# A Fourier layer folded by the symmetry of cosine and sine

## The chip, the cores and the metric

The program runs on one core of one Trainium2 chip. A core has five engines that matter here: TensorE (PE, matrix products, its weight loads shown apart as PEld), VectorE (DVE), ScalarE (ACT), GpSimd (POOL) and the queue that issues most DMAs (SP). Each runs its own list of instructions strictly in the order in which it was written at build time; between engines they wait by semaphores. The metric is the device time of one execution in microseconds, lower is better.

## The reference

Two layers on x of 512 tokens by 1024 channels in float32. Layer 0 mixes by attention and a recurrence, layer 1 by a Fourier transform over tokens and over the 256 channels of each of four groups. Each mixer is followed by a gated feed-forward of width 2816.

```python
def fourier_mixer(h, w):
    B, S, D = h.shape
    g = h.astype(jnp.float32).reshape(B, S, FOURIER_GROUPS, FOURIER_GROUP_DIM)
    f = jnp.fft.fft2(g, axes=(1, 3), norm='ortho').real
    return f.reshape(B, S, D).astype(h.dtype) @ w

def swiglu(h, wg, wu, wd):
    return (jax.nn.silu(h @ wg) * (h @ wu)) @ wd
...
    for l in range(DEPTH):
        hn = rmsnorm(x, ln_mix_pre[l])
        ...
        else:
            m = fourier_mixer(hn, w_fourier_out[l // 2])
        x = x + rmsnorm(m, ln_mix_post[l])
        hn = rmsnorm(x, ln_ffn_pre[l])
        x = x + rmsnorm(swiglu(hn, w_ffn_gate[l], w_ffn_up[l], w_ffn_down[l]), ln_ffn_post[l])
    return x
```

## The kernel before

Every float32 operand is split into a high and a low part of 12 significant bits (`split`, L100: the high part is a cast on ACT, the low part a subtraction on DVE), and every product is three matrix products, high by high, high by low and low by high (`mm3`, L109 to L111). A token tile is 128 tokens, so there are four (t = 0 to 3); a channel tile is 128 channels.

Weights come through one list of units of 256 columns or rows (`units`), each loaded as two halves of 512 KB by SP into one of three raw buffers (`raws`), then split (L103 on ACT, L106 on DVE) into tiles of a pool of 33 tiles of 128 x 1024 that everything else shares. `next_unit(ahead)` hands out a unit and has the following ones loaded and split. PSUM has eight banks of 128 x 512.

The stages in order are layer 0's mixer and output projection, FFN0, the Fourier mixer, and FFN1. `proj_tok` computes a product as [token, channel]: the row tiles of the contraction in chunks for all four token tiles, and the last of them, the tail, token tile by token tile, so that one token tile ends early and its norm runs beside the products of the next. `post_norm` (L255 to L266) takes the square sums on ACT, the root on POOL (`inv_sqrt`, L209) and the scaling and the residual sum on DVE; `pre_norm` (L236 to L242) normalises the new x, and `turn_x` transposes it on PE for the feed-forward, which needs channels on partitions.

The Fourier mixer takes four steps. `pre_norm_tok` (L764 to L769), called at the end of each of FFN0's token tiles, scales x by its root and splits it. `pos_dft` (L809) transforms over the tokens: cosines in 257 columns, sines in 255. `ch_dft` (L828) transforms over a group's channels into E and O, and `mirror` (L841) makes the columns k and 512-k of the spectrum from E-O and E+O. Last, `proj_tok` multiplies by w_fourier_out, eight row tiles by 1024 channels, with a tail of six, and hands each token tile to `fin1` (both norms). FFN1's first pass (`col_tiles` with `halves`) then works in two halves of 256 tokens, and turns tiles 2 and 3 under them.

The order of each engine's list isn't written out by hand: the framework's scheduler decides it from the program order, the dependences and the buffers in its pools.

## Time and profile before

| | us |
|---|---|
| median of 3 runs | 1058.29 (1057.21 to 1058.57) |
| span of the profiled execution | 1056.6 |
| PE busy in it | 1032.2 |
| DVE, ACT, POOL busy | 480.4, 391.1, 100.3 |
| Fourier mixer, first position product to first product of FFN1 | 607.26 to 685.90 |

The span runs from the first to the last instruction of one execution, so it leaves out what lies around it in a run's time. In the profile a row reads: line, engine, operation, written tile, read tiles, their shapes, count, then busy time, mean length of one in ns, and the idle time ahead of it with what ended it. PE's products overlap, so the distance between two starts, not the length, is what one costs. A row of the timeline begins with its start and its length in us; a row of the window table has the length of the window, the busy time of PE, PEld, DVE, ACT and POOL with their counts, the granted clock, the DMA share and GB/s.

### The profile page before, as it was taken

To read this page: it belongs to the slowest core of one execution; us is meant where nothing else is said; L and a number is where in the kernel's file an instruction comes from. 1 tells how busy PE (TensorE), PEld (TensorE's weight loads), DVE (VectorE), ACT (ScalarE), POOL (GpSimd) and SP (SyncE) were. 2 spreads that over 40 slices of the span, in tenths; PEclk is the share of its full clock that TensorE was granted. 3 is DMA by queue.
4 is the path that set the end of the run, shared out by engine and by line. 5 is a ranking of instruction groups with operands and counts; after the bars stand their busy time and mean duration, and the time that the engine had idled before them with its cause. 6 is when DMAs were issued, how large, how long until landed. Compare 5 with 4: busy or idle time off the path is not lost.

```text
span 1056.6 us, 12277 instructions
## 1 busy us (share of the span) xinstructions
PE 1032.2 (98%) x4913; PEld 857.7 (81%) x4913; DVE 480.4 (45%) x760; ACT 391.1 (37%) x644; POOL 100.3 (9%) x94
## 2 busy tenths in 40 slices
...
GB/s 222 161 107 70 95 46 95 119 41 41 205 153 80 113 108 98 80 81 89 168 111 110 1 65 155 1 80 219 92 127 101 79 80 107 93 80 138 3 1 80
DMA packets 73123, 102.92 MB, mean 97 GB/s; under 512 B 3893, under 2 KB 61290, under 8 KB 73066
## 3 DMA queue, kind: packets, MB, share of 16 engines
...
q8 instruction: 38, 0.62, 0.2%
...
## 4 chain that ended last, share of the span: by engine, by line
PE 94%; DVE 3%; ACT 1%; DMA 1%; issue 1%; POOL 0%; SPq 0%; DVEq 0%; POOLq 0%; ACTq 0%
PE pc L110 15%; PE pc L109 15%; PE pc L111 15%; PE pj L111 10%; PE pj L109 10%; PE pj L110 10%; PE pqk L109 1%; PE psc L559 1%; PE pqk L110 1%; PE pqk L111 1%; PE psc L558 1%; DMA raw<-in_w_in_dram 1%; PE pT L250 1%; PE pyg L109 1%; PE pv L111 1%; PE put L109 1%
## 5 line engine op out<-in xcount | busy, mean ns | idle before, releaser
L106 DVE TENSOR_TENSOR wlo<-raw,whi 128x1024 fp32r<-128x1024 f32 x158 | 190.9, 1232 | 272.2 <-ACT whi L103 221.1
L110 PE MATMUL pc<-hnlo,whi 128*128 128x512 f32 (+1 forms) x768 | 285.1, 372 | 0.0
L109 PE MATMUL pc<-hnhi,whi 128*128 128x512 f32 (+1 forms) x768 | 284.6, 372 | 0.5 <-ACT hnhi L103 0.5
L111 PE MATMUL pc<-hnhi,wlo 128*128 128x512 f32 (+1 forms) x768 | 284.9, 371 | 0.0
L103 ACT CAST whi<-raw 128x1024 fp32r<-128x1024 f32 x164 | 167.4, 1049 | 125.2 <-PE pj L110 31.0
L109 PEld LDWEIGHTS pc<-hnhi,whi 128*128 128x128 f32 x768 | 144.2, 188 | 26.1 <-ACT hnhi L103 1.0
L111 PEld LDWEIGHTS pc<-hnhi,wlo 128*128 128x128 f32 x768 | 144.7, 188 | 25.1
L110 PEld LDWEIGHTS pc<-hnlo,whi 128*128 128x128 f32 x768 | 144.7, 188 | 25.0 <-DVE hnlo L106 0.4
L109 PE MATMUL pj<-whi,gs 128*128 128x512 f32 x352 | 136.9, 389 | 0.0
L110 PE MATMUL pj<-wlo,gs 128*128 128x512 f32 x352 | 136.9, 389 | 0.0
L111 PE MATMUL pj<-whi,gs 128*128 128x512 f32 x352 | 136.9, 389 | 0.0
L93 ACT ACTIVATE gated<-pc 128x512 f32<-128x512 f32 x44 | 26.2, 597 | 268.6 <-PE pc L111 268.6
L729 DVE TENSOR_TENSOR gated<-gated,pc 128x512 f32<-128x512 f32 x44 | 30.2, 686 | 111.4 <-PE pc L111 111.4
L111 PEld LDWEIGHTS pj<-whi,gs 128*128 128x128 f32 x352 | 66.1, 188 | 13.8
L110 PEld LDWEIGHTS pj<-wlo,gs 128*128 128x128 f32 x352 | 66.1, 188 | 13.8
L109 PEld LDWEIGHTS pj<-whi,gs 128*128 128x128 f32 x352 | 66.1, 188 | 13.6
L209 POOL TENSOR_TENSOR r<-m,mhalf 128x1 f32<-128x1 f32 x32 | 17.5, 547 | 552.2 <-DVE m L216 552.2
L260 ACT ACTIVATE y<-pj 128x512 f32<-128x512 f32 x32 | 19.1, 597 | 82.3 <-PE pj L111 82.3
L103 ACT CAST gs<-gated 128x512 fp32r<-128x512 f32 x44 | 25.3, 618 | 52.2 <-PE pj L110 32.2
L106 DVE TENSOR_TENSOR gs<-gated,gs 128x512 fp32r<-128x512 f32 x44 | 28.4, 685 | 31.3 <-ACT gs L103 31.3
L106 POOL TENSOR_TENSOR wlo<-raw,whi 128x1024 fp32r<-128x1024 f32 x12 | 29.7, 2484 | 47.9 <-ACT whi L103 46.8
L93 ACT ACTIVATE p<-p,mx 128x512 f32<-128x512 f32 x32 | 23.1, 723 | 17.6 <-DVE mx L563 17.5
...
## 6 DMA issues: line engine op xcount, KB each, us to landing
raw<-in_w_ffn_gate_dram SPq DMA_DIRECT2D x44, 512.0 KB, 4.1
raw<-in_w_ffn_up_dram SPq DMA_DIRECT2D x44, 512.0 KB, 5.1
raw<-in_w_ffn_down_dram SPq DMA_DIRECT2D x44, 512.0 KB, 3.8
raw<-in_w_in_dram SPq DMA_DIRECT2D x20, 512.0 KB, 3.7
raw<-in_w_mix_out_dram SPq DMA_DIRECT2D x8, 512.0 KB, 3.3
raw<-in_w_fourier_out_dram SPq DMA_DIRECT2D x8, 512.0 KB, 4.3
pos<-in_dft_pos_dram POOLq DMA_DIRECT2D x8, 256.0 KB, 5.7
out_dram<-x SPq DMA_DIRECT2D x8, 256.0 KB, 2.1
```

The costliest lines, as they stand in the source:

```text
L93: ins = A.activation(out_, in_, func, **kw)
L103: A.copy(hi, src)
L106: lo_eng.tensor_tensor(out=lo, in0=src, in1=f(hi), op=ALU.subtract)
L109: T.matmul(ps, lhsT=l[0], rhs=r[0], start=start, stop=False)
L110: T.matmul(ps, lhsT=l[0], rhs=r[1], start=False, stop=False)
L111: T.matmul(ps, lhsT=l[1], rhs=r[0], start=False, stop=stop)
L209: G.tensor_tensor(out=r, in0=m, in1=mhalf[:, 0:1], op=ALU.pow)
L250: T.transpose(pt[:, k * P:(k + 1) * P], xh[:, k * P:(k + 1) * P], ident)
L260: A.activation(ys[h], ps[h], AF.Square, accum_out=ss[h])
L558: T.matmul(ps, lhsT=q_[m][:, t * P:(t + 1) * P], rhs=k_[m], start=True, stop=False)
L559: T.matmul(ps, lhsT=q_[m][sl, t * P:(t + 1) * P], rhs=klo[sl, :], start=False, stop=True)
L729: V.tensor_tensor(out=gated[fc], in0=gated[fc], in1=ps, op=ALU.mult)
```

## The change

The Fourier mixer is computed in a folded form. Cosine is even and sine odd, so within a group channels c and 256-c are combined first, as sums (for the cosines) and differences (for the sines). Rows j and 256-j of w_fourier_out are folded alike (`prep_folded`: the mirrored rows come by a gather DMA, sums and differences are made on DVE and both are split). The map is computed for tokens 0 to 255 as S (from the sums) and T (from the differences); tokens k and 512-k are S-T and S+T (`map_out`). Token tiles 2 and 3 of x are therefore kept in reversed order: written to a scratch in DRAM, gathered back, and stored to the output by a scatter. What doesn't fit the folding (channels 0 and 128, tokens 0 and 256) goes through small products (`pos_rest`, `ch_rest`, `map_rest`) and a row `acc` made on DVE. The gain `g1` of the pre-norm is now a row on all partitions, applied in `pre_norm_tok`. FFN1's first pass is `wide`: six column tiles in halves in place of four.

```diff
 def pre_norm_tok(t):
-        r = pre_stats(t, pair("junk"))
+        h = tile1k("h")
+        r = pre_stats(t, (h[:, 0:S], h[:, S:2 * S]))
+        V.scalar_tensor_tensor(out=h, in0=xt[t], scalar=r, in1=g_pre1[0], op0=ALU.mult, op1=ALU.mult)
+        hv = h.rearrange("p (g c) -> p g c", c=256)
+        w = tile1k("w")
+        wv = w.rearrange("p (z g c) -> p z g c", g=4, c=P)
+        V.tensor_copy(wv[:, :, :, 0:1].rearrange("p z g c -> p g (z c)"), hv[:, :, 0:256:P])
+        V.tensor_tensor(out=wv[:, 0, :, 1:P], in0=hv[:, :, 1:P], in1=hv[:, :, 255:P:-1], op=ALU.add)
+        G.tensor_tensor(out=wv[:, 1, :, 1:P], in0=hv[:, :, 1:P], in1=hv[:, :, 255:P:-1], op=ALU.subtract)
         hi = hn["hi"][:, 2 * t:2 * t + 2, :].rearrange("p a b -> p (a b)")
         lo = hn["lo"][:, 2 * t:2 * t + 2, :].rearrange("p a b -> p (a b)")
-        A.activation(hi, xt[t], AF.Copy, scale=r)
-        V.scalar_tensor_tensor(out=lo, in0=xt[t], scalar=r, in1=f(hi), op0=ALU.mult, op1=ALU.subtract)
-        xs[t] = (hi, lo)
+        for z in range(2):
+            sl = slice(z * S, (z + 1) * S)
+            split(hi[:, sl], lo[:, sl], w[:, sl])
+        hf[t] = (hi, lo)
...
+    def row_index(name, base, first):
+        ix = const.tile([P, 1], mybir.dt.int32, name="ix" + name)
+        G.iota(ix, pattern=[[0, 1]], base=base, channel_multiplier=-1)
+        G.memset(ix[0:1, :], first)
+        rowx[name] = bass.IndirectOffsetOnAxis(ap=ix, axis=0)
+    def gather(tile_, rows_, ix):
+        G.indirect_dma_start(out=tile_, out_offset=None, in_=rows_, in_offset=ix)
+    wsum = []
+    def prep_folded(ap, halves):
+        a, b = (raws.tile([P, 1024], F32, name=nm("raw"), tag="raw") for _ in range(2))
+        nc.sync.dma_start(a, ap[0:P, :])
+        gather(b, w_fourier_out, rowx["w%d" % len(wsum)])
+        G.memset(b[0:1, :], 0.0)
+        for op in (ALU.add, ALU.subtract):
+            w = tile1k("wf")
+            V.tensor_tensor(out=w, in0=a, in1=b, op=op)
+            if op == ALU.add:
+                wsum.append(w)
+            hi, lo = tile1k("whi", F32R), tile1k("wlo", F32R)
+            split(hi, lo, w)
+            halves.append((hi, lo))
...
+        if t >= 2:
+            nc.sync.dma_start(scratch[(t - 2) * P:(t - 1) * P, :], xt[t])
...
-    for n in range(2):
-        w = tile1k("ch", F32R)
-        G.dma_start(w, dft_ch[n])
-        chT.append(w)
+    chT = [tile1k("ch", F32R) for _ in range(2)]
+    def chw(i):
+        return chT[i // 8][:, (i % 8) * P:(i % 8 + 1) * P]
+    for z in range(2):
+        for n in range(2):
+            G.dma_start(chw(2 * z + n), dft_ch[n, :, z * 256:z * 256 + P])
+    G.memset(f(chT[0][:, S:]), 0.0)
+    G.memset(f(chT[1]), 0.0)
+    for g in range(4):
+        G.dma_start(chw(4 + g)[32 * g:32 * g + 1, :], dft_ch[0, 0:1, 512:512 + P])
+        for q in range(3):
+            G.dma_start(chw(8 + g)[:, 32 * q + g:32 * q + g + 1], dft_ch[0, :, P:P + 1])
+        G.memset(f(chw(12)[32 * g:32 * g + 1, g:g + 65:32]), 1.0 / 16.0)
+    G.memset(f(chw(13)[:, 0:1]), 1.0)
+    xr = [xt[0], xpool.tile([P, D], F32, name=nm("x2"), tag="x2"), xpool.tile([P, D], F32, name=nm("x3"), tag="x3"), xt[1]]
+    gather(xr[1], scratch, rowx["c"])
+    gather(xr[2], scratch, rowx["d"])
...
+    def pos_dft(g, ts):
+        if g not in ups:
+            ups[g] = bank("put")
+        ps = ups[g]
+        for t in ts:
+            for z, (r0, o0, n) in enumerate(((0, 0, 258), (257, 256, 256))):
+                o = (z * 4 + g) * P
+                mm3(ps[:, o0:o0 + n], [a[:, o:o + P] for a in hf[t]], [a[:, r0:r0 + n] for a in posT[t]],
+                    t == 0 and z == 0, t == 3 and z == 1, skip_group_check=True)
+    def pos_rest(ts):
+        if "r" not in ups:
+            ups["r"] = bank("put")
+        ps = ups["r"]
+        for t in ts:
+            mm3(ps[:, 0:258], [a[:, S:2 * S:4] for a in hf[t]],
+                [a[:, 0:258] for a in posT[t]], t == 0, t == 3)
...
+    def ch_dft(g):
+        pe, po = bank("pe"), bank("po")
+        ut, ur = uts[g], uts["r"]
+        mm3(pe[:, 0:258], (chw(0), chw(1)), [a[:, 0:258] for a in ut], True, False)
+        for a in ur:
+            T.matmul(pe[:, 0:258], lhsT=chw(4 + g), rhs=a[:, 0:258], start=False, stop=a is ur[1])
+        mm3(po[:, 0:256], (chw(2), chw(3)), [a[:, 256:512] for a in ut], True, True)
+        e, o = fe[g], fo[g] = pair("fe", F32R), pair("fo", F32R)
+        split(*[a[:, 0:256] for a in e], pe[:, 0:256])
+        e256[g] = sm("e256")
+        V.tensor_copy(e256[g], pe[:, 256:257])
+        for a in o:
+            G.memset(f(a[:, 0:1]), 0.0)
+        split(*[a[:, 1:256] for a in o], po[:, 1:256])
...
+    def ch_rest():
+        ps = bank("pe")
+        n = 0
+        for g in (0, 1, 2, 3, "r"):
+            for a in uts[g]:
+                T.matmul(ps[:, 0:258], lhsT=chw(8 + (4 if g == "r" else g)), rhs=a[:, 0:258], start=n == 0, stop=n == 9)
+                n += 1
+        e256["r"] = sm("e256")
+        V.tensor_copy(e256["r"], ps[:, 256:257])
+        A.copy(fr[:, 0:256], ps[:, 0:256])
+        V.tensor_tensor(out=fr[64:P, 0:256], in0=ps[64:P, 0:256], in1=f(fr[64:P, 0:256]), op=ALU.subtract)
...
-    proj_tok(range(8), lambda k: fT[k], 2, 6, fin1, turn_x)
+    acc = tile1k("acc")
+    V.tensor_scalar(out=acc, in0=wsum[0], scalar1=e256[0], scalar2=None, op0=ALU.mult)
+    for g in range(1, 4):
+        V.scalar_tensor_tensor(out=acc, in0=wsum[g], scalar=e256[g], in1=acc, op0=ALU.mult, op1=ALU.add)
+    V.scalar_tensor_tensor(out=acc[0:32, :], in0=w128[0:32, :], scalar=e256["r"][0:32, :], in1=acc[0:32, :], op0=ALU.mult, op1=ALU.add)
+    acch, accl = tile1k("acc", F32R), tile1k("acc", F32R)
+    split(acch, accl, acc)
+    psm = [[[bank("pm"), bank("pm")] for _ in range(2)] for _ in range(2)]
+    def map_part(i, h, g):
+        sl = slice(i * P, (i + 1) * P)
+        d = slice(h * S, (h + 1) * S)
+        ps = psm[i]
+        mm3(ps[0][h], [a[:, sl] for a in fe[g]], [a[:, d] for a in wf[g][0]], g == 0, False)
+        mm3(ps[1][h], [a[:, sl] for a in fo[g]], [a[:, d] for a in wf[g][1]], g == 0, g == 3 and i == 1)
+    def map_rest(i, h):
+        sl = slice(i * P, (i + 1) * P)
+        d = slice(h * S, (h + 1) * S)
+        T.matmul(psm[i][0][h], lhsT=fr[:, sl], rhs=wr[:, d], start=False, stop=True)
+        if i == 0:
+            for a in (acch, accl):
+                T.matmul(psm[i][1][h], lhsT=chw(13), rhs=a[:, d], start=False, stop=a is accl)
+    def map_out(i):
+        y = [pair("ya"), pair("yc")]
+        for h in range(2):
+            A.copy(y[0][h], psm[i][1][h])
+            V.tensor_tensor(out=y[1][h], in0=psm[i][0][h], in1=y[0][h], op=ALU.add)
+            V.tensor_tensor(out=y[0][h], in0=psm[i][0][h], in1=y[0][h], op=ALU.subtract)
+        for z in range(2):
+            t = (z, 3 - z)[i]
+            post_norm(t, y[z], g_post1)
+            pre_norm(t, g_fpre1)
+    for i in range(2):
+        for g in range(2):
+            for h in range(2):
+                map_part(i, h, g)
+    for i in range(2):
+        for h in range(2):
+            for g in (2, 3):
+                map_part(i, h, g)
+            map_rest(i, h)
+            if i and h:
+                turn_x(0)
+                turn_x(1)
+        map_out(i)
+    deferred.extend((lambda: turn_x(2), lambda: turn_x(3)))
...
+        if t in (1, 2):
+            G.indirect_dma_start(out=out, out_offset=rowx[("oc", "od")[t - 1]], in_=xt[t], in_offset=None)
+            return
...
-    ffn(1, after1, 4)
+    ffn(1, after1, 4, wide=True)
```

The change moves instructions on every engine. Three places follow, with the rows of each engine's list in their order (line, operation, written tile, read tiles, shape; x2 is two like rows).

**ACT at the end of FFN0.** Before: pj are the products of FFN0's token tiles, y the square of `post_norm`, junk that of `pre_norm_tok`, hnhi the high part of the normalised tile.

```order
L260 ACTIVATE y_4549,ss_4550<-pj_3923 128x512
L260 ACTIVATE y_4549,ss_4551<-pj_3924 128x512
L222 ACTIVATE junk_4566,ss_4567<-x_79 128x512
L222 ACTIVATE junk_4566,ss_4568<-x_79 128x512
L260 ACTIVATE y_4615,ss_4616<-pj_3925 128x512
L768 ACTIVATE hnhi_4564<-x_79,r_4575 128x1024
L260 ACTIVATE y_4615,ss_4617<-pj_3926 128x512
L222 ACTIVATE junk_4630,ss_4631<-x_80 128x512
L222 ACTIVATE junk_4630,ss_4632<-x_80 128x512
L260 ACTIVATE y_4679,ss_4680<-pj_3927 128x512
L768 ACTIVATE hnhi_4564<-x_80,r_4639 128x1024
```

After: h takes the place of junk, w holds the sums and differences of `pre_norm_tok`, of which the differences come from POOL (L827).

```order
L302 ACTIVATE y_4639,ss_4640<-pj_3949 128x512
L302 ACTIVATE y_4639,ss_4641<-pj_3950 128x512
L264 ACTIVATE h_4656,ss_4657<-x_81 128x512
L264 ACTIVATE h_4656,ss_4658<-x_81 128x512
L302 ACTIVATE y_4712,ss_4713<-pj_3951 128x512
L104 CAST hnhi_4654<-w_4668 128x512 x2
L302 ACTIVATE y_4712,ss_4714<-pj_3952 128x512
L264 ACTIVATE h_4727,ss_4728<-x_82 128x512
L264 ACTIVATE h_4727,ss_4729<-x_82 128x512
L302 ACTIVATE y_4783,ss_4784<-pj_3953 128x512
L104 CAST hnhi_4654<-w_4739 128x512 x2
L302 ACTIVATE y_4783,ss_4785<-pj_3954 128x512
```

The second square of y of the next tile stands behind the two high casts of the tile ahead of it, and those read w, which DVE and POOL have to finish first; before, it stood behind one cast that read x.

**POOL from the end of FFN0 on.** Before: r are roots of the norms, ch the constants of the channel transform, gpre a gain row.

```order
L209 TENSOR_TENSOR r_4688<-m_4685,mhalf 128x1
L209 TENSOR_TENSOR r_4703<-m_4700,mhalf 128x1
L209 TENSOR_TENSOR r_4752<-m_4749,mhalf 128x1
L116 DMA gpre_5105<-in_ln_ffn_pre_dram 128x1024
L799 DMA ch_4771<-in_dft_ch_dram 128x1024
L209 TENSOR_TENSOR r_4767<-m_4764,mhalf 128x1
L799 DMA ch_4773<-in_dft_ch_dram 128x1024
L209 TENSOR_TENSOR r_5234<-m_5231,mhalf 128x1
```

After (the first w is tile 2's difference, the second tile 3's; ch_4891 and ch_4892 are the constants, x_812 the gathered token tile).

```order
L827 TENSOR_TENSOR w_4810<-h_4798 128x4x127
L251 TENSOR_TENSOR r_4864<-m_4861,mhalf 128x1
L117 DMA gpost_5156<-in_ln_mix_post_dram 128x1024
L251 TENSOR_TENSOR r_4879<-m_4876,mhalf 128x1
L827 TENSOR_TENSOR w_4882<-h_4870 128x4x127
L881 DMA ch_4891<-in_dft_ch_dram 128x128 x4
L882 MEMSET ch_4891 128x512
L883 MEMSET ch_4892 128x1024
L885 DMA ch_4891<-in_dft_ch_dram 1x16x8
L887 DMA ch_4892<-in_dft_ch_dram 128x1 x3
L888 MEMSET ch_4892 1x3
L885 DMA ch_4891<-in_dft_ch_dram 1x16x8
```

The loads of the constants now stand behind the difference of the last tile; there are twenty of them, and 27 rows up to the first gather of x.

**DVE and PE at the entry of FFN1.** Before, on DVE: wlo_5168 to wlo_5192 are the low parts of FFN1's first two units; the m, y, x and xn rows are the norms of token tile 0.

```order
L106 TENSOR_TENSOR wlo_5168<-raw_5165,whi_5167 128x1024
L106 TENSOR_TENSOR wlo_5174<-raw_5171,whi_5173 128x1024
L106 TENSOR_TENSOR wlo_5186<-raw_5183,whi_5185 128x1024
L106 TENSOR_TENSOR wlo_5192<-raw_5189,whi_5191 128x1024
L215 TENSOR_SCALAR m_5230<-ss_5226 128x1
L216 TENSOR_SCALAR m_5231<-ss_5227,m_5230 128x1
L265 SCALAR_TENSOR_TENSOR y_5225<-pj_5109,r_5234,gpost_5103 128x512
L265 SCALAR_TENSOR_TENSOR y_5225<-pj_5110,r_5234,gpost_5103 128x512
L266 TENSOR_TENSOR x_79<-x_79,y_5225 128x512 x2
L215 TENSOR_SCALAR m_5245<-ss_5241 128x1
L216 TENSOR_SCALAR m_5246<-ss_5242,m_5245 128x1
L242 SCALAR_TENSOR_TENSOR xn_5240<-x_79,r_5249,gpre_5105 128x512 x2
```

After, on DVE: the norms of the last token tile (x_813), and behind them wlo_5477, the low part of FFN1's first half unit.

```order
L257 TENSOR_SCALAR m_5451<-ss_5447 128x1
L258 TENSOR_SCALAR m_5452<-ss_5448,m_5451 128x1
L307 SCALAR_TENSOR_TENSOR y_5446<-yc_5411,r_5455,gpost_5156 128x512 x2
L308 TENSOR_TENSOR x_813_4921<-x_813_4921,y_5446 128x512 x2
L257 TENSOR_SCALAR m_5466<-ss_5462 128x1
L258 TENSOR_SCALAR m_5467<-ss_5463,m_5466 128x1
L284 SCALAR_TENSOR_TENSOR xn_5461<-x_813_4921,r_5470,gpre_5158 128x512 x2
L107 TENSOR_TENSOR wlo_5477<-raw_5474,whi_5476 128x1024
L107 TENSOR_TENSOR wlo_5483<-raw_5480,whi_5482 128x1024
L107 TENSOR_TENSOR wlo_5489<-raw_5486,whi_5488 128x1024
```

The four splits that stood ahead of the norms now stand behind the norms of all four token tiles. On PE, before, the last product of the projection (pj) and the first of FFN1 (pc):

```order
L109 MATMUL pj_5116<-whi_5006,f_5100 128x512
L110 MATMUL pj_5116<-wlo_5007,f_5100 128x512
L111 MATMUL pj_5116<-whi_5006,f_5100 128x512
L109 MATMUL pc_5473<-hnhi_5107,whi_5167 128x256
L110 MATMUL pc_5473<-hnlo_5108,whi_5167 128x256
L111 MATMUL pc_5473<-hnhi_5107,wlo_5168 128x256
```

On PE, after, the end of the map (pm), with the row acc, and the first of FFN1:

```order
L1009 MATMUL pm_5209<-acc_5202,ch_4892 128x512
L1009 MATMUL pm_5208<-acc_5203,ch_4892 128x512
L1009 MATMUL pm_5209<-acc_5203,ch_4892 128x512
L292 MATMUL pT_5382<-ident,xn_5315 128x128 x4
L292 MATMUL pT_5389<-ident,xn_5315 128x128 x4
L292 MATMUL pT_5396<-ident,xn_5343 128x128 x4
L292 MATMUL pT_5403<-ident,xn_5343 128x128 x4
L110 MATMUL pc_5510<-hnhi_5160,whi_5476 128x256
L111 MATMUL pc_5510<-hnlo_5161,whi_5476 128x256
L110 MATMUL pc_5511<-hnhi_5160,whi_5476 128x256
L111 MATMUL pc_5511<-hnlo_5161,whi_5476 128x256
L112 MATMUL pc_5510<-hnhi_5160,wlo_5477 128x256
```

The products with acc stand at the end of the map, the turns pT of tiles 0 and 1 stand between the map and FFN1, and pc's third kind of product (L112) waits for wlo_5477.

149 lines of the change are left out of this document (81 added, 68 removed).

## The prediction

> **What bounds the kernel now.** I read the page's busy times first, then the chain that ended last, then the window table of the stage that changes.
>
> ```profile
> PE 1032.2 (98%) x4913; PEld 857.7 (81%) x4913; DVE 480.4 (45%) x760; ACT 391.1 (37%) x644; POOL 100.3 (9%) x94
> PE 94%; DVE 3%; ACT 1%; DMA 1%; issue 1%; POOL 0%; SPq 0%; DVEq 0%; POOLq 0%; ACTq 0%
> 606.00:622.00 16.00, 16.00 (x73) 13.23 (x72) 6.72 (x12) 5.25 (x11) 2.74 (x5) 1.00 0.32 99
> 622.00:645.00 23.00, 23.00 (x148) 20.98 (x147) 19.83 (x35) 16.93 (x35) 0.00 (x0) 1.00 0.30 93
> 645.00:660.00 15.00, 15.00 (x68) 12.43 (x67) 5.52 (x6) 4.68 (x7) 0.00 (x0) 1.00 0.46 140
> 660.00:700.00 40.00, 39.76 (x239) 35.22 (x238) 22.66 (x46) 13.75 (x38) 4.94 (x9) 1.00 0.04 14
> ```
>
> TensorE (PE) is the chain, and in the Fourier stage (window columns: length, then PE, PEld, DVE, ACT, POOL) it is busy without a gap. So each product removed is worth its step, but only as long as PE still finds its operands: DVE is busy for 19.83 of 23 us in the second window already.
>
> **What the arithmetic saves.** The step from one product to the next is read off PE's timeline (start, length).
>
> ```profile
> 607.26 0.39 PE L109 MATMUL put<-pos,hnhi 128*128 128x512 f32 x1
> 607.48 0.39 PE L110 MATMUL put<-pos,hnhi 128*128 128x512 f32 x1
> ...
> 623.58 0.28 PE L109 MATMUL pe<-u,ch 128*128 128x258 f32 x1
> 623.69 0.28 PE L110 MATMUL pe<-u,ch 128*128 128x258 f32 x1
> ...
> 685.68 0.39 PE L111 MATMUL pj<-whi,f 128*128 128x512 f32 x1
> 685.90 0.28 PE L109 MATMUL pc<-hnhi,whi 128*128 128x256 f32 x1
> ```
>
> A 512-column product takes 0.227 us, a 256- or 258-column one 0.12. Before: 96 x 0.227 + 96 x 0.12 + 192 x 0.227 = 76.9 us. After: positions 96 + 12 and channels 32 + 10 of at most 258 columns, 150 x 0.12 = 18.0, and the map's 96 + 8 of 512 columns, 23.6; together 41.6. PE is spared **35.3 us**. The wide first pass of FFN1 adds back 48 products' worth of halves: 96 x 0.12 - 48 x 0.227 = 0.6.
>
> **What the other engines add.** These rows price the new work (mean ns of one).
>
> ```profile
> L106 DVE TENSOR_TENSOR wlo<-raw,whi 128x1024 fp32r<-128x1024 f32 x158 | 190.9, 1232 | 272.2 <-ACT whi L103 221.1 <-issue 40.3 <-PE pc L110 10.4
> L769 DVE SCALAR_TENSOR_TENSOR hnlo<-x,r,hnhi 128x1024 fp32r<-128x1024 f32 x4 | 5.1, 1284 | 7.7 <-ACT hnhi L768 7.7
> L106 DVE TENSOR_TENSOR hnlo<-pT,hnhi 128x512 fp32r<-128x512 f32 x24 | 15.5, 682 | 9.3 <-ACT hnhi L103 9.3
> L488 DVE TENSOR_SCALAR gate<-th 128x512 f32<-128x512 f32 x8 | 3.1, 428 | 0.0
> L103 ACT CAST whi<-raw 128x1024 fp32r<-128x1024 f32 x164 | 167.4, 1049 | 125.2 <-PE pj L110 31.0 <-DMA raw<-in_w_ffn_gate_dram 23.9 <-PE pj L111 21.4
> L103 ACT CAST hnhi<-pT 128x512 fp32r<-128x512 f32 x24 | 13.2, 583 | 16.6 <-PE pT L250 16.6
> L497 POOL TENSOR_TENSOR gate<-gate,th 128x512 f32<-128x512 f32 x8 | 16.2, 2062 | 8.6 <-ACT th L93 8.6
> L471 POOL TENSOR_TENSOR gate<-gate,xc 128x512 f32<-128x512 f32 x8 | 12.3, 1557 | 36.2 <-ACT gate L93 36.2
> L789 POOL DMA_DIRECT2D pos<-in_dft_pos_dram x4 | 2.1, 528 | 278.4 <-PE pj L111 266.6 <-DVE gs L106 11.9
> ...
> masks.py:197 POOL MEMSET ident<- 128x128 f32 x1 | 0.2, 205 | 0.3 <-POOLq L915 0.3
> ```
>
> And the last norm before FFN1, from the timelines of ACT, POOL and DVE:
>
> ```profile
> 686.16 0.60 ACT L260 ACTIVATE y<-pj 128x512 f32<-128x512 f32 x1 [2.42 <-PE pj L111]
> ...
> 691.66 0.56 POOL L209 TENSOR_TENSOR r<-m,mhalf 128x1 f32<-128x1 f32 x1 [1.55 <-DVE m L216]
> ...
> 692.25 1.42 DVE L242 SCALAR_TENSOR_TENSOR xn<-x,r,gpre 128x512 f32<-128x512 f32 x2 [0.75 <-POOL r L209]
> ```
>
> From the start of the second square of y, the second root r is done after 6.1 us and the normalised tile after 7.5.
>
> **Step 1, into the Fourier stage.** FFN0's products still end near 607.3, as before; I put 0.8 on top, since four casts of gs now stand behind a weight cast that waits for PE. In the new order the last token tiles' tails are 24 products each (four row tiles, two halves, three), not 36, so tile 0 ends 3 x 24 x 0.227 = 16.3 us ahead of that, at 591.8; its second square starts at about 592.5. ACT's rows in the section on the change show what follows: tile t+1's second square stands behind tile t's two hi casts, and these wait for the difference on POOL (L827). One turn is 6.1 (to r) + 1.28 (h, as L769) + POOL's subtraction of 508 elements + two casts at 0.58. The subtraction lies between 1.56 and 2.06 by the two POOL rows; I take 1.8, their middle. That gives 10.3 us a tile, so tile 3's second square starts at 623.4, POOL's last subtraction ends at 632.7, and its halves are split by 634.6. Before, nothing there waited: the norms hid behind products that are now spent. PE's own products up to there (tiles 0 to 2: 72 and 9) are 81 x 0.12 = 9.7 us of the 26.5 after 608.1, so it idles about **17 us**.
>
> In the Trainium skill, "SBUF — State Buffer", Who interferes with whom, says that a DVE instruction with two SBUF inputs contends with a GpSimd instruction that reads SBUF, and that the loser blocks for the whole instruction. L826 (DVE) and L827 (POOL) are such a pair, so by it I would add up to one 0.68 per tile, 2.7 in all; the two POOL rows above already span 0.5 us for one shape, so the sum keeps their middle.
>
> **Step 2, the channel constants.** POOL's rows show its 20 ch loads and two wide memsets behind the last L827, where before the two loads stood among the norms. From 632.7: four loads at 0.55, memsets of 512 and 1024 elements (bounds: 0.2 each by the 128-element row, 1.6 by that row times eight; I take 1.2 for both), then four groups of four loads and a memset at 2.3: the last is issued at 645.3.
>
> ```profile
> lv<-in_lambda_q_dram SPq DMA_DIRECT2D x2, 32.0 KB, 3.4
> lv<-in_lambda_k_dram SPq DMA_DIRECT2D x2, 32.0 KB, 5.0
> raw<-in_w_fourier_out_dram SPq DMA_DIRECT2D x8, 512.0 KB, 4.3
> pos<-in_dft_pos_dram POOLq DMA_DIRECT2D x8, 256.0 KB, 5.7
> ```
>
> Landing takes 3.4 to 5.7 by the nearest rows (3.4 taken, the smallest load's), so ch_rest's products start at 648.7 and end at 650. DVE's copy of e256 from them stands ahead of the sum wf of weight unit 2: wf, lo, wf, lo at 1.23, with ACT's 1.05 casts between, run to 656.8. The second wf ends at 654.5 and frees the raws, and only then unit 3 loads (4.3, plus 0.55 to issue its gather; a gather is not in the trace, so 3.3 to 5.7). Its wf, cast, lo, wf, cast, lo end at 666.5. The accumulator row follows on DVE: one 0.86 (twice L488) and four of 1.28, then cast and lo: 674.8. PE's order has the four acc products after every other product of the map, so the map ends at **E = 675**. PE itself needs only 23.6 us for it.
>
> **Step 3, into FFN1.** This is the largest term. Before, tiles 0 to 2 were normalised under the products of the tiles behind them, FFN1's first weights were split ahead of the norms, and the first FFN1 product followed the last pj after 0.22 us (rows at 685.68 and 685.90). After, all four token tiles come out of the same last products, and DVE's rows show the first lo of FFN1 (wlo_5477) behind the fourth xn. From E: two copies from PSUM and the sums and differences, then the chain of tile 0, 10.5; tile 1 behind it 7.5; tile 3, with its own four sums and differences and tile 0's and 1's hnlo between, 10; tile 2, 7; wlo 1.2. That is 36.2, and PE does some 2 us of turns and four products within it. The DVE work alone bounds it from below: 8 x 0.68 for sums, per tile 2 x (0.75 + 0.68 + 0.75) and 0.36, four hnlo of 0.68 and one wlo are 28 us; waits between engines at the same hops, up to 40. FFN1 resumes at 711.2 instead of 685.9: **25.3 us later**, though PE had 35.3 less to do. Its later weights keep up: three raws are loaded by then, and a half unit costs DVE 1.23 against 24 x 0.12 = 2.9 of products.
>
> ```profile
> L242 DVE SCALAR_TENSOR_TENSOR xn<-x,r,gpre 128x512 f32<-128x512 f32 x24 | 17.0, 749 | 10.5 <-POOL r L209 7.1 <-DMA gpre<-in_ln_mix_pre_dram 3.2
> L265 DVE SCALAR_TENSOR_TENSOR y<-pj,r,gpost 128x512 f32<-128x512 f32 x32 | 22.6, 747 | 11.2 <-POOL r L209 11.2
> L266 DVE TENSOR_TENSOR x<-x,y 128x512 f32<-128x512 f32 x32 | 20.5, 682 | 0.0
> 13.00:18.00 5.00, 4.27 (x18) 3.98 (x19) 4.22 (x8) 3.69 (x8) 0.56 (x1) 1.00 0.85 301
> ...
> 13.53 0.41 PE L110 MATMUL pv<-wlo,hnhi 128*128 128x256 f32 x1
> ...
> 17.46 0.41 PE L109 MATMUL pv<-whi,hnhi 128*128 128x256 f32 x1
> 17.68 0.41 PE L110 MATMUL pv<-wlo,hnhi 128*128 128x256 f32 x1
> ...
> 18.10 0.28 PE L109 MATMUL pv<-whi,hnhi 128*128 128x256 f32 x1
> 18.22 0.28 PE L110 MATMUL pv<-wlo,hnhi 128*128 128x256 f32 x1
> ```
>
> The last six rows are the kernel's own start. The window's granted clock reads 1.00 there, yet from 13.53 to 18.10 a 256-column product steps by 0.22 us and from then on by 0.12. Those 4.6 us do the work of 2.5, so I add **2 us** for the same after the long idle (0 to 2.1). The Trainium skill, "TensorE: Matmul & The Clock Gate", Part 1: The HAM clock gate, states half clock after an idle window and about 3.4 us of work to leave it; by its figure I would estimate 1.7 here, and nothing at the shorter gaps where PE waits for a norm anyway.
>
> The remaining edits cost nothing that PE waits for: the iotas lie at the start, ahead of a wait for the first DMAs; the x2 and x3 rows go out on SP during the norms and are gathered some 20 us before map_out reads them; the scattered stores of tiles 1 and 2 lie beside the tail's products, and tile 3 still leaves through SP. If that cover fails, each is one transfer of 4 to 6 us by the two rows of 512 and 256 KB above.
>
> **The sum.** 25.3 + 0.6 + 2 - 0.5 (four FFN1 products done early) = 27.4. The profiled span is 1056.6 us and the median of the runs 1058.29, so 1.7 lies around it: 1084.0 as a span, **1085.7** as a time, 2.6% slower.
>
> **The rivals.**
> - *The arithmetic decides, faster.* Were every wait hidden, 1058.3 - 35.3 + 0.6 = 1023.6. It needs the new idle time to stay below 35 us; steps 1 and 3 alone make 17 and 34. Its place is FFN1's entry: it decides where the four norms end behind running products again, so that step 3's 36.2 shrink below 10. For it speaks only that DVE and ACT are under half busy over the span. 0.08.
> - *FFN1 starts on two tiles.* If PE resumed when tiles 0 and 1 are turned (E + 20) and the second pair ran under FFN1's first half, it would be 16 us earlier, 1069. DVE's order speaks against it; a weight split that comes earlier than its row would be needed. 0.12.
> - *POOL's loads are slower, still slower than forecast.* 12 loads of one element per partition and three gathers have no like in the trace. At 5.7 instead of 3.4 to land, and 1 us instead of 0.55 to issue, step 2 grows by 2.3 + 20 x 0.45 = 11.3: 1097. It decides once E depends on ch_rest, as it does here by 650. 0.15.
> - *It does not do what it says.* If 258-column products with strided weights cost the 512-column step, 150 x 0.107 = 16 us come back, mostly in idle time: up to 1095. The ch rows, already 258 wide at 0.12, speak against it. 0.03.
>
> The forecast has 0.62 (its own range 1074 to 1096). To hold 8 in 10, the range reaches to the second and third rivals: 1066 to 1100. About 0.2% is what a measurement here can tell from no change: faster 0.08, within it 0.03, slower 0.89.
>
> **What would show it.** Right: PE waits at the Fourier entry for hnhi casts in turns of about 10 us; POOL busy with issues until 645; acc the last map products at 675; DVE busy and PE empty for over 30 us before pc, released by wlo. Wrong: pc starting while post-norms still run, POOL's subtraction or loads far off the rows, or PE without gaps in the first 30 us after FFN0.

## The result, and the profile after

| | before | after |
|---|---|---|
| median of four runs each, us | 1058.43 (1057.21 to 1059.18) | 1089.15 (1088.79 to 1091.72) |
| ratio to before | | 1.0298 (1.0283 to 1.0313) |
| span of the profiled execution, us | 1056.6 | 1089.9 |
| PE busy in it, us | 1032.2 | 1015.0 |

The changed kernel is 3.0% slower. The profiled execution of after is the slowest of its four runs (1091.72), so 2.6 us of its span are not in the median.

First the page of after: busy time, share of the span and instructions of each engine, then PE's busy tenths in 40 slices of 27.2 us and the clock granted to it.

```profile
PE 1015.0 (93%) x4831; PEld 843.5 (77%) x4831; DVE 501.5 (46%) x786; ACT 387.6 (36%) x636; POOL 143.0 (13%) x201
...
PE   5999999999999999999999777179999999999997
...
PEclk9998999999999999999999989579999999999999
```

PE is busy 17.2 us less, yet the span is 33.3 longer, so PE's idle time has grown by 50.5 us. The slices say where: from the 23rd to the 27th, 599 to 736 us, and worst in the 26th, 681 to 708, where PE is busy for a tenth and the clock falls to 5 tenths. The window table shows two stretches of it (length, then PE, PEld, DVE, ACT, POOL, clock, DMA share, GB/s):

```profile
608.00:640.00 32.00, 19.69 (x105) 18.41 (x104) 18.56 (x38) 10.72 (x28) 12.71 (x16) 0.83 0.20 58
...
680.00:720.00 40.00, 9.51 (x40) 8.45 (x41) 29.39 (x55) 17.60 (x44) 5.04 (x9) 0.50 0.12 36
```

Before, PE was busy in every microsecond from 606 to 660. Now 12 of 32 us are missing in the first window, and 30 of 40 between 680 and 720, where DVE works 29.39 us and the granted clock is 0.50. PE's timeline of after names the waits (start, length, row, then the idle time ahead of it and what ended it):

```profile
609.98 0.28 PE L110 MATMUL put<-pos,hnhi 128*128 128x258 f32 x1
...
615.50 0.36 PE L110 MATMUL put<-pos,hnhi 128*128 128x258 f32 x1 [4.63 <-issue]
...
625.98 0.61 PE L110 MATMUL put<-pos,hnhi 128*128 128x258 f32 x1 [1.89 <-ACT hnhi L104]
...
636.77 0.60 PE L110 MATMUL put<-pos,hnhi 128*128 128x258 f32 x1 [5.57 <-ACT hnhi L104]
...
651.68 0.50 PE L110 MATMUL pm<-whi,fo 128*128 128x512 f32 x1 [0.57 <-POOL fo L949]
...
677.51 2.48 PE L1009 MATMUL pm<-acc,ch 128*128 128x512 f32 x4 [4.21 <-ACT acc L104]
689.70 1.94 PE L292 MATMUL pT<-ident,xn 128*128 128x128 f32 x8 [9.71 <-DVE xn L284]
696.80 1.97 PE L292 MATMUL pT<-ident,xn 128*128 128x128 f32 x8 [5.16 <-DVE xn L284]
713.01 0.58 PE L110 MATMUL pc<-hnhi,whi 128*128 128x256 f32 x1 [14.25 <-ACT whi L104]
...
715.62 0.58 PE L112 MATMUL pc<-hnhi,wlo 128*128 128x256 f32 x1 [1.38 <-DVE wlo L107]
```

PE waits in turns for the high part hnhi of the next tile, then for acc, for the normalised tiles xn, and for the first high and low part of a weight (whi, wlo). The row at 615.50 names no releaser, but ACT's casts of tile 1's hnhi end 0.1 us ahead of it (614.26 and 1.14 us). These rows give the books of the stage. From the first position product (609.98) to the third product of FFN1 (715.62) pass 105.6 us, of which PE needs 41.6 by the prediction's count. The other 64 us lie in four stretches ("lost" is the length less the products' own time; it holds waits and slow steps):

| stretch | from, to | length | products | lost |
|---|---|---|---|---|
| token tiles 0 to 2, waiting for tile 3 | 609.98, 636.77 | 26.8 | 81 of 0.12 | 17.1 |
| tile 3, channel transform, first map products | 636.77, 651.68 | 14.9 | 69 of 0.12, 6 of 0.227 | 5.3 |
| rest of the map, with the products of acc | 651.68, 679.99 | 28.3 | 98 of 0.227 | 6.1 |
| norms and turns ahead of FFN1 | 679.99, 715.62 | 35.6 | (four, and the turns) | 35.6 |

The stage began 2.7 us later than before (607.26) and released FFN1's third product 29.5 later (686.13 before, two steps behind 685.90). From there to the end of the span 374.3 us pass, 370.5 before.

### The profile page after: what moved, and what is told of

It is laid out like the page before. It is cut to its first block, busy times and chain, and to the rows that moved or that the text cites. A ratio compares the mean times of both kernels' runs of the same rounds, so it can differ in the third digit from the quotient of the medians.

```text
span 1089.9 us, 12286 instructions
## 1 busy us (share of the span) xinstructions
PE 1015.0 (93%) x4831; PEld 843.5 (77%) x4831; DVE 501.5 (46%) x786; ACT 387.6 (36%) x636; POOL 143.0 (13%) x201
## 5 line engine op out<-in xcount | busy, mean ns | idle before, releaser
L107 DVE TENSOR_TENSOR wlo<-raw,whi 128x1024 fp32r<-128x1024 f32 x150 | 181.4, 1232 | 263.9 <-ACT whi L104 218.8
L110 PE MATMUL pc<-hnhi,whi 128*128 128x512 f32 (+1 forms) x784 | 288.6, 370 | 14.6 <-ACT whi L104 14.2
L112 PE MATMUL pc<-hnhi,wlo 128*128 128x512 f32 (+1 forms) x784 | 289.0, 369 | 1.4 <-DVE wlo L107 1.4
L104 ACT CAST whi<-raw 128x1024 fp32r<-128x1024 f32 x156 | 159.5, 1049 | 119.2 <-PE pj L111 33.5
L110 PEld LDWEIGHTS pc<-hnhi,whi 128*128 128x128 f32 x784 | 148.7, 190 | 39.6 <-ACT whi L104 14.6
L112 PEld LDWEIGHTS pc<-hnhi,wlo 128*128 128x128 f32 x784 | 149.1, 190 | 26.1 <-DVE wlo L107 1.7
L111 PEld LDWEIGHTS pc<-hnlo,whi 128*128 128x128 f32 x784 | 149.4, 191 | 24.4 <-DVE hnlo L107 0.2
L112 PE MATMUL pj<-whi,gs 128*128 128x512 f32 x352 | 136.2, 390 | 0.0
L110 PEld LDWEIGHTS pj<-whi,gs 128*128 128x128 f32 x352 | 66.1, 188 | 15.7 <-ACT gs L104 2.2
L112 PEld LDWEIGHTS pj<-whi,gs 128*128 128x128 f32 x352 | 66.1, 188 | 14.4 <-DVE gs L107 0.7
L858 POOL DMA_DIRECT2D pos<-in_dft_pos_dram x8 | 4.5, 566 | 270.9 <-PE pj L112 263.1
L292 PE MATMUL pT<-ident,xn 128*128 128x128 f32 x96 | 15.7, 313 | 26.0 <-DVE xn L284 25.1
L302 ACT ACTIVATE y<-pj 128x512 f32<-128x512 f32 x24 | 14.3, 595 | 62.4 <-PE pj L112 62.4
```

What stands on the lines that cost most here:

```text
L104: A.copy(hi, src)
L107: lo_eng.tensor_tensor(out=lo, in0=src, in1=f(hi), op=ALU.subtract)
L110: T.matmul(ps, lhsT=l[0], rhs=r[0], start=start, stop=False, **kw)
L111: T.matmul(ps, lhsT=l[0], rhs=r[1], start=False, stop=False, **kw)
L112: T.matmul(ps, lhsT=l[1], rhs=r[0], start=False, stop=stop, **kw)
L292: T.transpose(pt[:, k * P:(k + 1) * P], xh[:, k * P:(k + 1) * P], ident)
```

## The experiments

The theory: the arithmetic is saved as counted, but the order of the program sets three serial chains in its place, one at the entry (a norm per token tile), one at the map's end (acc behind the last folded weights), one ahead of FFN1 (four norms, and only then the first split of a weight). Its rivals: that an edit of another kind costs the time (the wide pass, the buffers), and that DVE's sheer work, not the order, fills the gap. All times are medians, with the ratio to the kernel before on the same chip. That kernel took 1059.00 us beside e1 to e4, 1058.57 beside e5 to e8 and 1058.77 beside e9 to e11, against 1058.43 beside the change, so differences between kernels hold to 1 or 2 us.

| kernel | median, us | ratio |
|---|---|---|
| e1: acc left out | 1084.10 | 1.0240 (1.0223 to 1.0257) |
| e2: two units split ahead | 1080.97 | 1.0205 (1.0188 to 1.0222) |
| e3: differences on DVE | 1084.34 | 1.0243 (1.0226 to 1.0260) |
| e5: norms in pairs | 1088.07 | 1.0278 (1.0262 to 1.0293) |
| e6: first pass not wide | 1088.60 | 1.0280 (1.0264 to 1.0295) |
| e4: all three chains mended | 1056.91 | 0.9985 (0.9976 to 0.9995) |
| e7: e4, norms in pairs, one low part on POOL | 1054.18 | 0.9955 (0.9942 to 0.9969) |
| e8: before, with four raw buffers | 1059.75 | 1.0009 (1.0000 to 1.0018) |
| e9: e7, not wide | 1063.97 | 1.0049 (1.0032 to 1.0065) |
| e10: e7, splits not ahead | 1069.85 | 1.0107 (1.0091 to 1.0124) |
| e11: e7, entry as changed | 1065.17 | 1.0058 (1.0041 to 1.0075) |

### One chain at a time

**e1** leaves out the row acc and its four products.

```diff
-    acc = tile1k("acc")
...
-    split(acch, accl, acc)
...
-        if i == 0:
-            for a in (acch, accl):
-                T.matmul(psm[i][1][h], lhsT=chw(13), rhs=a[:, d], start=False, stop=a is accl)
```

> Leaves out the row acc: its five DVE operations, its cast and low part, and its four products (the output of tokens 0 and 256 lacks their term). Theory (the map's end waits for acc): in the profile of the changed kernel PE has done every other product of the map by 673.3 and waits 4.21 us for acc, whose products end at 679.5. Without them the map ends about 6 us earlier and the time is 1089 - 6 = 1083 (1081 to 1085). Rival (the map's end is set by the weights of unit 3 alone and acc lies beside them): 1088 to 1089.5.

It came out at 1084.1: acc, last in the map's order, costs about 5 us. In its profile the map ends at 675.41 instead of 679.99, although tile 3's first product comes 2.1 us later than in after (638.90), for a reason that wasn't tried; so 5 us may be somewhat too little.

**e2** splits FFN1's first two units ahead of the last products of the map, so that they stand ahead of the four norms on ACT and DVE.

```diff
+    for _ in range(2):
+        prep_one()
     for i in range(2):
         for h in range(2):
             for g in (2, 3):
                 map_part(i, h, g)
```

> Hands out FFN1's first two units ahead of the map's end in the program, so that their four splits stand ahead of the first copy of map_out on ACT and DVE. Theory (PE waits at FFN1's entry for a weight split that stands behind four norms): tiles 0 and 1 were normalised at 697.4, the split came at 715.6. The fourth raw can be loaded only when the first split frees its buffer (about 680), lands 4 to 5 us later, and the copies behind its cast start at 685.5 instead of 679.6, so the norms come 6 us later: products of FFN1 resume at about 705, and the rest of the first half waits a little for the third unit. 1089 - 9 = 1080 (1077 to 1083). Rival (the norms of all four tiles are needed before FFN1 can work): no gain or a loss, 1089 to 1095.

It came out at 1080.97, 8 us less than the change. PE's timeline of e2:

```profile
695.38 1.94 PE L292 MATMUL pT<-ident,xn 128*128 128x128 f32 x8 [15.83 <-DVE xn L284]
702.48 1.97 PE L292 MATMUL pT<-ident,xn 128*128 128x128 f32 x8 [5.16 <-DVE xn L284]
704.27 1.01 PE L110 MATMUL pc<-hnhi,whi 128*128 128x256 f32 x3
...
718.70 0.39 PE L110 MATMUL pc<-hnhi,whi 128*128 128x256 f32 x1 [1.64 <-ACT whi L104]
```

The first turn is now 5.7 us later than in after (689.70), since DVE does four splits first, but FFN1 follows the second turn directly, at 704.27: the 14.25 us of idle time ahead of 713.01 in after are gone. Those were an order, not a lack of an engine.

**e3** moves the differences of the entry from POOL to DVE.

```diff
-        G.tensor_tensor(out=wv[:, 1, :, 1:P], in0=hv[:, :, 1:P], in1=hv[:, :, 255:P:-1], op=ALU.subtract)
+        V.tensor_tensor(out=wv[:, 1, :, 1:P], in0=hv[:, :, 1:P], in1=hv[:, :, 255:P:-1], op=ALU.subtract)
```

> The difference of channels c and 256-c (L827) on DVE instead of POOL. Theory (the turn of 10.3 to 11.1 us per token tile into the Fourier stage is one chain through POOL's 1.8 us): sum and difference take 2 x 0.68 on DVE, and the first high cast need not wait for the second; each of four tiles gains about 1.0, the turn is 9.5, and all behind it moves with it: 1089 - 4 = 1085 (1084 to 1087). By the Trainium skill's page on SBUF, where a DVE instruction with two SBUF inputs blocks beside a GpSimd one, the gain would be larger by what POOL loses to DVE now. Rival (the entry is bound by FFN0's products or by the constants on POOL): 1088 to 1090.

It came out at 1084.34. DVE's timeline of e3 shows one turn of the chain and the next:

```profile
608.41 1.29 DVE L821 SCALAR_TENSOR_TENSOR h<-x,r,gpre 128x1024 f32<-128x1024 f32 x1 [0.73 <-POOL r L251]
...
609.81 0.68 DVE L826 TENSOR_TENSOR w<-h 128x508 f32<-128x508 f32 x1
610.41 0.68 DVE L827 TENSOR_TENSOR w<-h 128x508 f32<-128x508 f32 x1
...
617.94 1.29 DVE L821 SCALAR_TENSOR_TENSOR h<-x,r,gpre 128x1024 f32<-128x1024 f32 x1 [0.73 <-POOL r L251]
```

The difference takes 0.68 us here against 1.79 on POOL, and a turn 9.5 us (608.41 to 617.94) against the 10.3 to 11.1 of after. ACT's order changed with it (both squares of the next tile stand ahead of the high casts), so the gain isn't the 1.1 us of the instruction alone. PE gets tile 3 at 630.46 instead of 636.77; 1.4 of these 6.3 us lie ahead of the stage (first position product at 608.56 instead of 609.98). The spans of the two profiled executions differ by 9.2 us, twice the 4.8 of the medians, so times read off one execution can't be set against a median to the microsecond.

**e6** takes the wide first pass back.

```diff
-    ffn(1, after1, 4, wide=True)
+    ffn(1, after1, 4)
```

> FFN1's first pass in halves over four column tiles again, not six; all else as in the changed kernel. Theory (PE resumes only behind all four norms, so the wide pass covers nothing here and only costs its halves): 48 products of 512 columns in place of 96 of 256 save 0.6, and the third unit is needed later: 1089 - 0.6 = 1088.4 (1086.5 to 1089.2). Rival (the wide pass covers the norms of tiles 2 and 3, as it is built to): 1092 to 1096.

At 1088.6 it can't be told from the change: where FFN1 starts with all weights late, the wide pass buys nothing.

### A miss: the norms in pairs

**e5** writes the two norms of `map_out` stage by stage, so that each engine finds the second token tile's step beside the first's.

```diff
-        for z in range(2):
-            t = (z, 3 - z)[i]
-            post_norm(t, y[z], g_post1)
-            pre_norm(t, g_fpre1)
+        for z in range(2):
...
+            rs.append(inv_rms(ss[0], ss[1], D))
+        for z in range(2):
+            for h in range(2):
...
+                V.tensor_tensor(out=xt[ts[z]][:, sl], in0=xt[ts[z]][:, sl], in1=ys[z][h], op=ALU.add)
+        for z in range(2):
+            xs2[z] = pair("xn")
+            rs[z] = pre_stats(ts[z], xs2[z])
...
```

> In map_out alone, the norms of the two token tiles of a half are written stage by stage (both squares and roots, then both residual sums, and so on) instead of one tile behind the other; nothing else differs from the changed kernel. Theory (the 36 us from the map's end to FFN1 are one in-order chain on DVE, part of it waits for roots and squares): in the changed kernel DVE is idle for about 8 of the 35 us between its first sum (680.22) and the split (715.58), in waits of 0.2 to 0.75; in pairs about half of them are covered by the other tile. 1089 - 4.5 = 1084.5 (1082 to 1087). Rival (DVE's and ACT's work itself fills the chain): 1088 to 1090.

It came out at 1088.07, where the rival had it. The window of e5 from the end of the map to the first low part of FFN1, and PE's timeline:

```profile
679.10:712.60 33.50, 5.01 (x20) 4.05 (x20) 26.73 (x54) 17.12 (x43) 7.00 (x9) 0.55 0.05 16
```

```profile
691.23 1.94 PE L292 MATMUL pT<-ident,xn 128*128 128x128 f32 x8 [12.32 <-DVE m L257]
693.40 1.84 PE L292 MATMUL pT<-ident,xn 128*128 128x128 f32 x8 [0.23 <-DVE xn L1042]
...
712.64 0.58 PE L112 MATMUL pc<-hnhi,wlo 128*128 128x256 f32 x1 [2.97 <-DVE wlo L107]
```

DVE works 26.73 of these 33.5 us (27.56 of 36 in after, 680 to 716), so pairing can only squeeze the 7 us in which it waits, and it took two of them. The first turn comes later (691.23 against 689.70), the second at once behind it. So for the chain ahead of FFN1 both theories hold a part: DVE's work fills it, and only the order decides whether PE has products meanwhile.

### All three mended

**e4** mends the three chains at once. The gain is applied to x before the root is known, and the root goes into the high cast and the low part, as before the change; the differences are on DVE; the term of acc goes to PE as 26 products (column 256 as one more column of each left operand) in place of a row made on DVE; three units are split ahead of the map's end, with a fourth raw buffer and one tile less in the pool; the loads of pos come later.

```diff
-NTILE = 33
-NRAW = 3
+NTILE = 32
+NRAW = 4
...
-        V.scalar_tensor_tensor(out=h, in0=xt[t], scalar=r, in1=g_pre1[0], op0=ALU.mult, op1=ALU.mult)
+        V.tensor_tensor(out=h, in0=xt[t], in1=g_pre1[0], op=ALU.mult)
...
-            split(hi[:, sl], lo[:, sl], w[:, sl])
+            A.activation(hi[:, sl], w[:, sl], AF.Copy, scale=r)
+            V.scalar_tensor_tensor(out=lo[:, sl], in0=w[:, sl], scalar=r, in1=f(hi[:, sl]), op0=ALU.mult, op1=ALU.subtract)
...
-        if k < 4 and calls[0] >= 32 + 4 * k:
+        if k < 4 and calls[0] >= 40 + 8 * k:
...
+        if i == 0:
+            mm3(ps[1][h], [a[:, 256:384] for a in fe[g]], [a[:, d] for a in wf[g][0]], False, False)
...
+            T.matmul(psm[i][1][h], lhsT=fr[:, 256:384], rhs=wr[:, d], start=False, stop=True)
...
+    for _ in range(3):
+        prep_one()
```

> Same result by another order of the same work: the gain is multiplied to x before the root is known and the root applied in the high and low parts; the difference on DVE; acc as 26 products on PE (column 256 as a further column tile) instead of a DVE row; four raw buffers and 32 tiles instead of three and 33; the position loads 8 hook calls later; six splits of FFN1 ahead of map_out. Theory (the three waits are independent and add up): entry 4 x 2 to 3 us, acc and unit 3's late raw 6 + 4, FFN1's entry 9 to 16, less 22 x 0.227 = 5 for the added products where PE isn't idle: 1089 - 30 = 1059 (1050 to 1066), about the time of the kernel before. Rival (another wait takes their place, DVE being the bound of the whole stage): 1070 to 1080.

At 1056.91 it is some 32 us below the change, more than the 18 that e1 to e3 gained one by one (5.1, 8.2 and 4.8; by the ratios 33 against 22). e4 also does more at each place than they do: six splits ahead instead of four, the gain ahead of the root, the later loads.

**e7** adds the pairs of e5 to e4 and gives the low parts of one more unit of FFN1 to POOL.

```diff
-LO_POOL = (8,9,10,11,12,13)
+LO_POOL = (8,9,10,11,12,13,54)
```

> The kernel of e4 with the norms in pairs as in e5, and the low parts of FFN1's third unit split on POOL. Theory (as e4, the next wait is tile 0's and 1's chain behind the map's end: in e4 PE stands idle for 6.9 and 5.16 us there): the second of the two waits goes and about 1 of the first: 1056.9 - 4.5 = 1052.4 (1050 to 1055). Rival (tiles 2 and 3 come later and the second half of the first pass waits for them instead): 1056 to 1058.

At 1054.18 it is the fastest kernel of this study, 0.45% under the one before; which of its two edits gave how much wasn't tried apart, nor whether they would make the kernel before faster as well, so that this lead is the folding's isn't shown. PE's timeline of e7, to be read against the rows of after above:

```profile
624.99 0.39 PE L110 MATMUL put<-pos,hnhi 128*128 128x258 f32 x1 [2.06 <-ACT hnhi L831]
...
675.95 1.94 PE L292 MATMUL pT<-ident,xn 128*128 128x128 f32 x8 [8.03 <-DVE m L257]
678.12 1.97 PE L292 MATMUL pT<-ident,xn 128*128 128x128 f32 x8 [0.23 <-DVE xn L1034]
679.91 1.22 PE L110 MATMUL pc<-hnhi,whi 128*128 128x256 f32 x4
```

Tile 3 comes 11.8 us earlier than in after, after a wait of 2.06 us, and FFN1 starts at 679.91, 6.0 us ahead of the kernel before. It still loses 8.03 us ahead of the first turn, and 2.2 of the 6.0 go again behind it (372.9 us from there to the end of the span, 370.7 before).

**e8** asks whether the fourth raw buffer (with one tile less) brings e4 and e7 below the kernel before.

```diff
-NTILE = 33
-NRAW = 3
+NTILE = 32
+NRAW = 4
```

> The kernel before the change with four raw buffers and 32 tiles, which e4 and e7 have too. Theory (PE is the bound there and hardly waits; 17 us of waits in all, none in the Fourier stage): 1058.3, between 1056 and 1059.5. Rival (e4's lead over the kernel before comes from the fourth raw buffer, not from the folding): 1054 to 1056.

It doesn't: 1059.75, level with the kernel before, and 0.25 us above the range that was expected.

### Each mend taken back from e7

**e9** takes the wide pass back (the edit of e6), **e10** the three `prep_one()` ahead, **e11** the entry (root before the gain, split from w, differences on POOL, as the change has them).

> The kernel of e7 with FFN1's first pass over four column tiles, not six (as e6, but where the splits stand first). Theory (the wide pass covers the norms of tiles 2 and 3 only where PE resumes on tiles 0 and 1): in e7 the first half begins at 679.9 and its 144 products cover the stretch to 698.8, just behind the second pair's norms (696.3). With 96 products it ends near 692.5 and PE waits about 5 to 8 us for the second pair: 1054.2 + 6 = 1060 (1057 to 1064). Rival (the wide pass is worth nothing here either, as in e6): 1053.5 to 1055.

> The kernel of e7 with FFN1's first units handed out behind map_out again, as in the change. Theory (this place of the splits is the largest single part of the loss): the splits come behind the fourth norm, at about 697, instead of 655, and PE resumes near 697 instead of 679.9; nothing is left for the wide pass to cover: 1054.2 + 14 = 1068 (1064 to 1071). Rival (with the norms in pairs and the map early the splits' place matters little): 1055 to 1060.

> The kernel of e7 with pre_norm_tok as in the change: the gain is applied behind the root, and the difference comes from POOL. Theory (the turn of 10.3 to 11.1 us per token tile is on the path): tile 3's first product came at 624.99 in e7 and at 636.77 in the changed kernel; some of it is FFN0's end, which lies 2 earlier here: 1054.2 + 10 = 1064 (1061 to 1067). Rival (with the weights' sums or the constants as the next late thing the entry is covered): 1055 to 1058.

They lose 9.8, 15.7 and 11.0 us of e7. So the splits and the entry are worth 7.5 and 6.2 us more here than e2 and e3 gained alone, about the 14 that e4 had over the sum. But e10 takes back six splits where e2 moved four, and e11 the place of the gain beside the differences. That mending one chain shifts part of the wait to the next is shown for the splits, which in e2 delay the first turn by 5.7 us; for the entry it isn't, and what part of the 14 us it makes is open. In e11 the entry's delay passes on in full: tile 3's first product comes 9.95 us later than in e7 (634.94) and FFN1's first 11.1 (691.02). The third chain (acc as products on PE) and the later loads of pos weren't taken back. PE's timeline of e9 and of e10 where it happens:

```profile
696.25 1.94 PE L292 MATMUL pT<-ident,xn 128*128 128x128 f32 x8 [9.36 <-DVE xn L1034]
```

```profile
689.90 0.58 PE L110 MATMUL pc<-hnhi,whi 128*128 128x256 f32 x1 [13.21 <-ACT whi L104]
...
694.09 0.58 PE L112 MATMUL pc<-hnhi,wlo 128*128 128x256 f32 x1 [2.97 <-DVE wlo L107]
```

In e10 PE waits 13.21 us with both turns done, until the first cast of a weight comes through, as in after. In e9 FFN1 starts in time but runs out of columns before the second pair is normalised, and waits 9.36 us for it: the wide pass is the cover for the second pair, and worth something only once FFN1 can start on the first. The change alone had the cover without that start.

## Why the prediction held, step by step

The direction and the size held: 1085.7 forecast, 1089.15 measured, inside the range. Of the 3.5 us between them, the steps account as follows (in the times of the profiled execution, whose span is 5.9 above the forecast 1084.0).

**The arithmetic.** 4831 products and turns instead of 4913, and the stage's 41.6 us of products stand in the table above as counted; the 82 fewer are the 130 saved less the 48 of the wide pass; the rival in which this decides (1023.6) needed the idle time under 35 us, and it is 64.

**Step 1, the entry.** FFN0's products end 2.7 us later, not 0.8: the first put starts at 609.98. This term was mis-sized. PE's one wait for a cast of gs, for which the 0.8 stood, is 0.8 in the trace of after; what makes the other 1.9 wasn't tried. The turn was priced at 10.3 us, and ACT's rows of after (second square of y of tiles 1 to 3, behind the two high casts) with POOL's last difference say:

```profile
603.62 1.14 ACT L104 CAST hnhi<-w 128x512 fp32r<-128x512 f32 x2 [3.59 <-POOL w L827]
604.66 0.59 ACT L302 ACTIVATE y<-pj 128x512 f32<-128x512 f32 x1
...
615.30 0.59 ACT L302 ACTIVATE y<-pj 128x512 f32<-128x512 f32 x1
...
626.36 0.59 ACT L302 ACTIVATE y<-pj 128x512 f32<-128x512 f32 x1
```

```profile
634.26 1.81 POOL L827 TENSOR_TENSOR w<-h 128x508 f32<-128x508 f32 x1 [1.49 <-DVE h L821]
...
646.63 1.62 POOL L887 DMA_DIRECT2D ch<-in_dft_ch_dram  x3
...
655.54 0.96 POOL L200 DMA_INDIRECT raw<-in_w_fourier_out_dram,ixw  x1 [3.12 <-DVE wf L212]
662.26 0.94 POOL L209 MEMSET raw<- 1x1024 f32 x1 [5.75 <-DMA raw<-in_w_fourier_out_dram,ixw]
```

Turns of 10.6 and 11.1 us, the last difference done at 636.07 instead of 632.7 (FFN0's 1.9 and 1.5 of the turns), and 17.1 us lost on PE against the 17 forecast. The difference took 1.81 us, with 1.8 chosen. Here the Trainium skill's "SBUF — State Buffer", Who interferes with whom, was weighed: by it the pair L826 and L827 contend, and one of them blocks. DVE's L826 takes 0.68 us beside POOL's L827 in after, and 0.68 with nothing on POOL in e3, so DVE didn't block. For POOL no run has L827 with DVE at rest, but another product of POOL on 128x512 tiles shows both cases (least, median and longest time in ns):

```profile
L514 POOL TENSOR_TENSOR gate<-gate,xc x8: 1290/1297/2282, 56.9 to 72.0; 128x512 f32<-128x512 f32 x8
```

The first two, from 56.89 us on, take 1.29 and 1.30 us, while DVE rests or reads one input from PSUM; the longest runs from 69.73 us on beside DVE's wlo<-raw,whi, which reads both from SBUF. So I estimate from these that about 0.5 of L827's 1.8 us is a wait for DVE; that L827 reads one input backwards may have a part in it. The two POOL rows of the forecast are means over such short and long ones, so that their middle came out right is luck.

**Step 2, the constants and acc.** The last ch load is issued by 648.25, 3 us later than forecast, as late as the entry. The DMA view of after, 640 to 670 us (queue, count, size where it is known, median us from issue to landing):

```profile
ch<-in_dft_ch_dram POOLq DMA_DIRECT2D x16, 0.5 KB, 1.9
x<-scratch,ixc POOLq DMA_INDIRECT x1, 4.5
...
raw<-in_w_fourier_out_dram,ixw POOLq DMA_INDIRECT x1, 6.7
```

The ch loads landed in 1.9 us, where 3.4 was taken from the nearest row, and only four of ch_rest's ten products waited for the last of them (649.70); together that gave the 3 us back but for a half, which is luck. The step that failed in size is the gather of the last folded unit, priced at 4.85 us with its issue (4.3 from a plain load, at most 5.7 without the issue): it took 6.7, and the memset of a row behind it, which the sum didn't have, 0.94 (POOL's row at 662.26). DVE's rows of after:

```profile
650.45 0.16 DVE L970 COPY e<-pe 128x1 f32<-128x1 f32 x1 [0.32 <-PE pe L967]
...
663.23 1.23 DVE L212 TENSOR_TENSOR wf<-raw,raw 128x1024 f32<-128x1024 f32 x1 [5.62 <-POOL raw L209]
...
677.49 1.22 DVE L107 TENSOR_TENSOR acc<-acc,acc 128x1024 fp32r<-128x1024 f32 x1 [1.17 <-ACT acc L104]
...
713.02 1.41 DVE L284 SCALAR_TENSOR_TENSOR xn<-x,r,gpre 128x512 f32<-128x512 f32 x2 [0.74 <-POOL r L251]
714.35 3.49 DVE L107 TENSOR_TENSOR wlo<-raw,whi 128x1024 fp32r<-128x1024 f32 x3
```

The copy of e256 starts at 650.45 (650 forecast), the first sum of unit 3 at 663.23 instead of 659.4, acc's low part ends at 678.7 instead of 674.8, and the map at 679.99 instead of 675: 0.5 us from the constants, 3.4 from unit 3, 1.1 from the last products, which had been put at 0.2. The order was as forecast, acc last, and e1 shows that this was worth 5 us.

**Step 3, into FFN1.** 36.2 us were forecast from E to the release of pc's third product by wlo, and it took 35.6 (679.99 to 715.62), with the last xn at 713.02 and wlo behind it on DVE, as its order had it. The 28 us of DVE work that bounded it from below are what e5 ran into. The rival in which FFN1 starts on two tiles didn't come, for the reason given against it; e2 and e7 make that kernel by placing the splits earlier; e2 gains 8 of the rival's 16 us, since its splits delay the norms.

**The clock.** 2 us were forecast for slower steps behind the long idle time. PE's timeline of after, behind 715.62:

```profile
716.22 0.41 PE L111 MATMUL pc<-hnlo,whi 128*128 128x256 f32 x1
716.43 0.41 PE L112 MATMUL pc<-hnhi,wlo 128*128 128x256 f32 x1
...
721.69 0.29 PE L112 MATMUL pc<-hnhi,wlo 128*128 128x256 f32 x1
721.82 0.28 PE L110 MATMUL pc<-hnhi,whi 128*128 128x256 f32 x1
```

The steps are 0.21 us until 721.5 and 0.12 from there on: 5.9 us do the work of 3.3, so 2.6. The Trainium skill, "TensorE: Matmul & The Clock Gate", Part 1: The HAM clock gate, gives about 3.4 us of sustained work at half clock, and says that the window runs freely. From that figure I would estimate a slow stretch of one to two windows, 3.4 to 6.8 us; the 5.9 measured lie within that, and the loss of 2.6 lies above the 1.7 that had been worked out from one window.

**The strided weights.** The last rival's condition holds, but for 12 products and not for 150. Only `pos_rest` takes its weights at a stride (every fourth column), and its products step by 0.235 us for 258 columns (622.51 to 623.69 in after), between neighbours of 0.12, with weight loads of 0.33 us against 0.19; in e7 they step by 0.235 as well (621.12 to 622.53). The ch rows that spoke against it have no stride. It costs some 1.4 us in all, nine of the twelve while PE waits for tile 3 anyway.

**The sum.** E is 5.0 later, the chain behind it 0.6 shorter, the clock 0.6 dearer, and PE waits another 0.97 us ahead of a turn at 737.14, inside FFN1's first pass: together 6.0 of the 5.9 by which the span is longer. That is the account of this one execution; the median lies 2.6 us below it, and which of these terms is smaller there can't be told. The wide pass, put at 0.6, can't be seen (e6). The rival with POOL's loads (1097) had the place but not the reason: POOL's plain loads were issued at 0.54 us each (1.62 for three), 0.55 priced, and only the gather was slow.
